# Four small edits to a one-core hybrid mixer block: where the last weights are loaded, a root, a store's queue, and the spacing of side steps

## The chip, the cores and the metric

The program runs on one core of one Trainium2 chip. The metric is the time of one execution on the device in microseconds; of several runs the median counts. The engines have their usual names: PE (TensorE, matmuls), DVE (VectorE), ACT (ScalarE), POOL (GpSimd) and SP, which here only issues DMAs. Each engine works through its own instructions in the order in which they stand in the program, and waits where an operand or a buffer is not ready.

## The reference, cut to what matters

One layer of a hybrid block over 512 latent tokens and 256 context tokens, width 2048, float32:

```
u  = (rms_norm(x)  * (1 + sc)   + sh)   @ w_in      # three head groups read one projection
uc = (rms_norm(ctx) * (1 + sc_c) + sh_c) @ w_in
y_gdn = gated DeltaNet, 6 heads, both directions    # chunked, a triangular solve in each chunk
y_hy  = order-2 Hyena, 512 channels, by FFT
y_ml  = mLSTM, 6 heads, both directions             # matrix memory with exponential gates
x = x + gt * (concat(y_gdn, y_hy, y_ml) @ w_out)    # gt: the gate, a third part of silu(c) @ mod_w
out = x * rsqrt(mean(x * x, -1) + 1e-6) * final_norm
```

## The kernel before

The big products are done at float32 accuracy from halves: a weight tile `raw` (128 x 512) is split into `whi` (a rounded copy by ACT, L275) and `wlo` (the rest, by DVE, L276), and each product is three matmuls of 128 x 512: `xh*whi`, `xl*whi` and `xh*wlo` (L418 to L420; with 256 context columns L427 to L429; in the output projection L1769 to L1771). `raw` has three buffers (RB = 3), `whi` and `wlo` three each (WB = 3). SP issues the load of a piece (L362) when a `raw` buffer is free, that is when the `wlo` of three pieces before is done.

**The middle.** The input projection is a stream of such products, the fill. `weave` (L843) puts the small steps of four chains between them: `gdn` (the DeltaNet heads), `ml_scans` (the mLSTM heads), `gates_row` (the gate) and `convs` (Hyena). A chain yields a pair: the clock units that its step is worth, and the units to wait until its next step. The units are the planner's own clock; a K tile of fill, three matmuls of 512 columns, is worth 0.65. So a pause of LX = 0.5 puts one K tile of fill between two steps, and a pause of 2.0 some four. The planner fixes an order of instructions; it does not see the chip. In `ml_scan` a head of the mLSTM begins with transposes of `kT` and `vT` into PSUM banks of the tag `s` (two buffers), which ACT copies to SBUF (L1486, to `kt` and `v1`, shown as `v`). Then come four scores (L1497, again in `s` banks; ACT takes the exponential, L1500, and DVE the product PT, L1501), then twelve scan steps (L1515 to L1519, in banks of the tag `st`, of which there are three). The solve of the DeltaNet's head runs at the same time; its small DMAs (`mblk`, `ublk`) are issued by ACT, between ACT's activations. It also takes `s` banks: for the transposes of its `vT` (L1364, copied out by ACT as `vr`, L1366), for the 32 x 32 and 64 x 64 products of the inverse. Its scan (L1386, L1393, L1402, L1415) takes two `st` banks at a time. `residual_gate` sums sixteen tiles into `gacc` on DVE (L1571), four times over, and closes each sum with a matmul by a column of ones (L1574).

**The end.** The output projection goes by four blocks of 512 columns, cb = 0 to 3; block 0 is the last of the weave. In blocks 1 and 2 the loop runs over the sixteen K tiles and inside it over four token tiles, so that a piece of weights serves four products. In block 3 the loop runs over the token tiles outside and the K tiles inside, so its sixteen pieces must all be there: thirteen lie in a pool of their own (`wq`), three in the usual buffers. They are drawn from the generator `last_cols`, and before they were drawn in block 2, one behind each K tile 1 to 12, the last four behind the block. `residual` adds the residual, squares it on ACT with a sum over the row into `ss`, and multiplies by the final norm's weights. In block 3 each token tile is closed at once: the sum of squares, its root by `rsqrt1` on DVE (a shift and a subtraction of the bits, then three Newton steps on a tile of 128 x 1), four scalings by ACT and DVE, and four stores of 256 KB by SP (L1855).

Of the kernel before, what the change touches and what calls it, by code (L numbers as in the profile page):

```python
# [10 lines left out]
F32 = mybir.dt.float32  # L11
# [28 lines left out]
LD = 3.5  # L40
LM = 0.5
LX = 0.5
LC = 6.0
LM0 = 1.0
LK = 8.0
# [179 lines left out]
def block_kernel(ctx: ExitStack, tc: tile.TileContext, io, out, dbg=None):  # L225
# [29 lines left out]
    def p_s():  # L255
        return bank("s", 2)
# [83 lines left out]

    def rsqrt1(pool, y, v, tag, bufs):

        i = pool.tile([128, 1], I32, tag=tag, bufs=bufs, name="rs_i")
        DVE.tensor_single_scalar(out=i, in_=v.bitcast(I32), scalar=1, op=ALU.arith_shift_right)
        DVE.tensor_scalar(out=i, in0=i, scalar1=-1, scalar2=0x5F3759DF, op0=ALU.mult, op1=ALU.add)
        w = i.bitcast(F32)
        t = pool.tile([128, 1], F32, tag=tag, bufs=bufs, name="rs_t")
        for c in (3.0, 12.0, 768.0):
            DVE.scalar_tensor_tensor(out=t, in0=w, scalar=v, in1=w, op0=ALU.mult, op1=ALU.mult)
            DVE.scalar_tensor_tensor(out=y, in0=t, scalar=-c, in1=w, op0=ALU.add, op1=ALU.mult)  # L350
            w = y
        DVE.tensor_single_scalar(out=y, in_=y, scalar=-1.0 / 8192, op=ALU.mult)


    wcount = [0]
# [1115 lines left out]
    def ml_scan(h, kT, vT, qT, oT):  # L1471
# [9 lines left out]
        for src, dst in ((kT, kt), (vT, v1)):  # L1481
            for t0, n in ((0, 4), (4, 2)):
                pt = p_s()
                for t in range(n):
                    PE.transpose(pt[:, 128 * t:128 * t + 128], src[:, 128 * (t0 + t):128 * (t0 + t) + 128], ident)
                ACT.activation(out=dst[:, t0:t0 + n, 0:128], in_=pt[:, :128 * n].rearrange("p (t c) -> p t c", c=128),  # L1486
                               func=AF.Copy)
                yield 0.15 * n, LX
        for d in range(2):
            s_ = 1 if d == 0 else -1  # L1490
            paced(POOL.affine_select(out=rows[d], in_=rows[d], pattern=[[0, NL], [s_, 128]], base=0,
# [2 lines left out]
        for j in range(NL):  # L1494
            t = j + NC_
            pk = p_s()
            PE.matmul(pk[:, 0:128], kT[:, 128 * t:128 * t + 128], qT[:, 128 * j:128 * j + 128], start=True, stop=True)  # L1497
            for d in range(2):
                ex = s1.tile([128, 128], F32, tag="ex", bufs=2, name="ex")
                ACT.activation(out=ex, in_=rows[d][:, j], func=AF.Exp, bias=am[:, t, 6 * d + h:6 * d + h + 1])  # L1500
                DVE.tensor_tensor(out=PT[:, d, j], in0=pk[:, 0:128], in1=ex, op=ALU.mult)  # L1501
            yield 0.22, LX
        o_sb = s1.tile([128, NL, 128], F32, tag="mosb", bufs=1, name="osb")
        Cn = [None, None]
        for n in range(NT):
# [53 lines left out]
    def residual_gate():  # L1559

        for b in range(4):
            acc = se.tile([128, 512], F32, tag="gacc", name="gacc")
            for j in range(KT):
                m = wp.tile([128, 512], F32, tag="raw", bufs=RB, name="mg")
                SP.dma_start(out=m, in_=io["mg"][b, j // 2, :, 512 * (j % 2):512 * (j % 2) + 512])
                yield 0, LD
                sk = scol[:, j:j + 1]
                if j == 0:
                    paced(DVE.tensor_single_scalar(out=acc, in_=m, scalar=sk, op=ALU.mult))
                else:  # L1570
                    paced(DVE.scalar_tensor_tensor(out=acc, in0=m, scalar=sk, in1=acc, op0=ALU.mult, op1=ALU.add))  # L1571
                yield 0, LG - LD
            pg = p_s()
            PE.matmul(pg[0:1], ones[:, 0:1], acc, start=True, stop=True)  # L1574
            m = wp.tile([128, 512], F32, tag="raw", bufs=RB, name="mbt")
            SP.dma_start(out=m[0:1], in_=io["mbg"][:, 512 * b:512 * b + 512])
            DVE.tensor_tensor(out=m[0:1], in0=pg[0:1], in1=m[0:1], op=ALU.add)
            SP.dma_start(out=gt_d[:, 512 * b:512 * b + 512], in_=m[0:1])
            yield 0.9, LG
# [227 lines left out]
    fnb = s3.tile([128, D], F32, name="fnb")  # L1807
    POOL.dma_start(out=fnb, in_=io["fnw"].to_broadcast([128, D]))
    ss = s3.tile([128, NL, 4], F32, name="ss3")

    def residual(o, t, cb):
        cs = slice(512 * cb, 512 * cb + 512)
# [5 lines left out]
        ACT.activation(out=xt, in_=rs, func=AF.Square, accum_out=ss[:, t, cb:cb + 1])  # L1818
        if cb < 3:
            DVE.tensor_tensor(out=rs, in0=rs, in1=fnb[:, cs], op=ALU.mult)  # L1820

    wq = outs.enter_context(tc.tile_pool(name="wq", bufs=KT - WB, side="right", reuse_waits="tile"))
    last_cols, ws = w_cols(3, wq), []
    for cb in range(3):
        pt = pt0 if cb == 0 else po_tiles(cb)
        if cb:
            for i, (k, w) in enumerate(zip(ks, w_cols(cb))):
                for t in range(NL):
                    y_product(pt[t], k, t, w)
                if cb == 2 and 0 < i < KT - WB:  # L1830
                    ws.append(next(last_cols))
        for t in range(NL):
            residual(pt[t], t, cb)
# [3 lines left out]
    for t in range(NL):  # L1837
# [2 lines left out]
            y_product(o, k, t, w)  # L1840
        residual(o, t, 3)
        v = s3.tile([128, 1], F32, tag="fv", bufs=2, name="fv")
        DVE.tensor_reduce(out=v, in_=ss[:, t], op=ALU.add, axis=AX.X)
        DVE.tensor_scalar(out=v, in0=v, scalar1=1.0 / D, scalar2=EPS, op0=ALU.mult, op1=ALU.add)
        r = s3.tile([128, 1], F32, tag="fr", bufs=2, name="fr")
        rsqrt1(s3, r, v, "fq", 4)
        for q in (0, 1, 3, 2):
# [4 lines left out]
                ACT.activation(out=rs, in_=rs, func=AF.Copy, scale=r)  # L1852
            else:
                DVE.tensor_single_scalar(out=rs, in_=rs, scalar=r, op=ALU.mult)
            SP.dma_start(out=out[128 * t:128 * t + 128, 512 * q:512 * q + 512], in_=rs)  # L1855
    outs.close()
    cxs.close()
    pss.close()
# [20 lines left out]
```

## Time and profile before

| | |
|---|---|
| median of three runs | 1495.4 us (1494.79 to 1498.05) |
| the profiled execution's own time | 1492.42 us |
| its span, first to last instruction | 1490.6 us |
| PE busy | 1445.4 us (97%) |
| DVE, ACT, POOL busy | 1031.0, 575.1, 215.0 us |
| granted clock of PE | 0.998 of full speed |

The profile is of one execution. Its own time is 1.8 us more than its span, which lies around the first and the last instruction, and 3.0 us less than the median of the runs. A row of PE gives the modelled time of a matmul from its first column in to its last result out, so rows of a stream overlap: the next one starts before the last has ended.

### The profile page before, as it was taken

Reading aid. Unit: us, or ns where it says so; the run is one execution under the profiler, and the core shown is the slowest. Engines: PE = TensorE matmul, PEld = TensorE weight load, DVE = VectorE, ACT = ScalarE, POOL = GpSimd, SP = SyncE. Lnnn points to the kernel's source line nnn. Section 1 sums busy time; section 2 is a strip of 40 time slices with the busy share of each in tenths; the row PEclk is TensorE's granted clock in tenths of the full one; section 3 lists DMA queues with packets and bytes.
Section 4 is the critical chain, followed back from the end, with each engine's and each line's share of the span. In section 5 each row is a group of like instructions: output and inputs, shape, how many; then the busy total and the mean of one; then the engine's idle time right before and its main releaser. Section 6 shows DMA issues by size and latency. Waiting matters only on the chain.

```text
span 1490.6 us, 25062 instructions
## 1 busy us (share of the span) xinstructions
PE 1445.4 (97%) x8822; PEld 1185.2 (80%) x8822; DVE 1031.0 (69%) x2685; ACT 575.1 (39%) x1367; POOL 215.0 (14%) x412
## 2 busy tenths in 40 slices
PE   5999999999999999999999999999999999999997
PEld 1565687888888888888888888888878888888775
DVE  4666776677778787878787767676776677774553
ACT  5433344425242624262335243533353333332431
POOL 2224002112010211020103001200011112210000
PEclk9999999999999999999999999999999999999999
DMA  9999623333344423442344123311322442474542
GB/s 320 318 315 298 218 81 100 102 104 100 100 140 113 123 95 120 125 127 92 124 129 133 65 83 94 110 55 60 86 79 88 163 167 95 149 240 142 169 125 101
DMA packets 145237, 202.82 MB, mean 136 GB/s; under 512 B 57222, under 2 KB 57703, under 8 KB 144856
## 3 DMA queue, kind: packets, MB, share of 16 engines
q1 hardware_dynamic: 89752, 159.50, 32.8%
q0 software_dynamic: 10048, 32.52, 6.9%
q10 hardware_dynamic: 45312, 9.21, 3.2%
q8 instruction: 69, 1.13, 0.3%
q14 instruction: 56, 0.46, 0.1%
HBM read 182.92 MB, written 18.26 MB: 135 GB/s over the span
## 4 chain that ended last, share of the span: by engine, by line
PE 77%; DVE 8%; issue 5%; DMA 5%; ACT 3%; POOL 1%; ACTq 0%; SPq 0%; DVEq 0%; POOLq 0%
PE ml L418 12%; PE ml L420 12%; PE ml L419 12%; PE mc L427 3%; PE mc L428 2%; PE mc L429 2%; PE st L317 2%; DVE wlo L276 2%; PE st L1771 1%; PE st L1770 1%; PE st L1769 1%; DMA raw<-in_wo_dram 1%; PE st L1393 1%; PE st L1402 1%; PE st L323 1%
## 5 line engine op out<-in xcount | busy, mean ns | idle before, releaser
L418 PE MATMUL ml<-xh,whi 128*128 128x512 f32 x1024 | 419.5, 410 | 0.0
L420 PE MATMUL ml<-xh,wlo 128*128 128x512 f32 x1024 | 404.7, 395 | 0.0
L419 PE MATMUL ml<-xs,whi 128*128 128x512 f32 x1024 | 404.5, 395 | 0.0
L275 ACT ACTIVATE whi<-raw 128x512 fp32r<-128x512 f32 x320 | 201.0, 629 | 427.5 <-PE mc L428 150.6
L276 DVE TENSOR_TENSOR wlo<-raw,whi 128x512 fp32r<-128x512 f32 x320 | 221.5, 694 | 177.8 <-ACT whi L275 165.6
L420 PEld LDWEIGHTS ml<-xh,wlo 128*128 128x128 f32 x1024 | 192.5, 188 | 38.9
L418 PEld LDWEIGHTS ml<-xh,whi 128*128 128x128 f32 x1024 | 193.4, 189 | 29.3 <-issue 0.9
L419 PEld LDWEIGHTS ml<-xs,whi 128*128 128x128 f32 x1024 | 193.3, 189 | 27.7
L427 PE MATMUL mc<-cs,whi 128*128 128x256 f32 x384 | 110.7, 288 | 0.0
L428 PE MATMUL mc<-cs,whi 128*128 128x256 f32 x384 | 108.6, 283 | 0.0
L429 PE MATMUL mc<-cs,wlo 128*128 128x256 f32 x384 | 108.3, 282 | 0.0
L427 PEld LDWEIGHTS mc<-cs,whi 128*128 128x128 f32 x384 | 72.6, 189 | 4.1 <-issue 0.9
L428 PEld LDWEIGHTS mc<-cs,whi 128*128 128x128 f32 x384 | 72.3, 188 | 3.1
L429 PEld LDWEIGHTS mc<-cs,wlo 128*128 128x128 f32 x384 | 72.8, 190 | 0.0
L1571 DVE SCALAR_TENSOR_TENSOR gacc<-mg,scol,gacc 128x512 f32<-128x512 f32 x60 | 45.5, 759 | 17.3 <-DMA mg<-in_mg_dram 9.0
L1288 POOL DMA_DIRECT2D G<-rows_d x36 | 19.8, 553 | 217.6 <-DVE T L1154 77.5
L1400 POOL TENSOR_SCALAR ke<-kt,kend 128x128 f32<-128x128 f32 x60 | 24.2, 408 | 150.4 <-PE st L1402 143.6
L1513 POOL TENSOR_SCALAR ke<-kt,wend 128x128 f32<-128x128 f32 x60 | 27.4, 459 | 94.5 <-ACT kt L1486 47.5
L1340 ACT ACTIVATE ex<-G,ngc 128x128 f32<-128x128 f32 x72 | 27.0, 398 | 33.5 <-POOL G L1295 14.3
L1770 PE MATMUL st<-wlo,yh 128*128 128x512 f32 x96 | 37.7, 392 | 0.0
L1771 PE MATMUL st<-whi,yl 128*128 128x512 f32 x96 | 37.7, 392 | 0.0
L1769 PE MATMUL st<-whi,yh 128*128 128x512 f32 x96 | 37.6, 391 | 0.0
(501 smaller groups left out, 2857.4 us busy)
## 6 DMA issues: line engine op xcount, KB each, us to landing
raw<-in_wt_dram SPq DMA_DIRECT2D x256, 256.0 KB, 2.8
mw<-in_mw_dram SPq DMA_DIRECT2D x128, 256.0 KB, 5.8
mg<-in_mg_dram SPq DMA_DIRECT2D x64, 256.0 KB, 2.8
raw<-in_wo_dram SPq DMA_DIRECT2D x64, 256.0 KB, 3.0
fraw<-in_wf_dram SPq DMA_DIRECT2D x16, 320.0 KB, 6.4
G<-rows_d POOLq DMA_DIRECT2D x36, 128.0 KB, 3.3
xs<-in_xT_dram SPq DMA_DIRECT2D x16, 256.0 KB, 5.4
hspec<-hv POOLq DMA_DIRECT2D x16, 256.0 KB, 5.4
```

The lines of the kernel that those rows point to most:

```text
L275: ACT.activation(out=hi, in_=src, func=AF.Copy)
L276: DVE.tensor_tensor(out=lo, in0=src, in1=hi.bitcast(F32), op=ALU.subtract)
L418: PE.matmul(pl[:m], wh, xh[:, kk], start=f, stop=False)
L419: PE.matmul(pl[:m], wh, xl[kk], start=False, stop=False)
L420: stream[0] = PE.matmul(pl[:m], wl, xh[:, kk], start=False, stop=l)
L427: PE.matmul(pc[:m, :CTX], wh, ch[kk], start=f, stop=False)
L428: PE.matmul(pc[:m, :CTX], wh, cl[kk], start=False, stop=False)
L429: stream[0] = PE.matmul(pc[:m, :CTX], wl, ch[kk], start=False, stop=l)
L1571: paced(DVE.scalar_tensor_tensor(out=acc, in0=m, scalar=sk, in1=acc, op0=ALU.mult, op1=ALU.add))
L1769: PE.matmul(o, yh[k][:, ts_], wh, start=f, stop=False)
L1770: PE.matmul(o, yh[k][:, ts_], wl, start=False, stop=False)
L1771: PE.matmul(o, yl[k][:, ts_], wh, start=False, stop=l)
```

## The change

- `last_cols`, the pieces of block 3, are drawn in blocks 1 and 2, behind every second K tile from the sixth on (i = 5, 7, ... 15), six in each block, twelve in all; four are left for the end of block 2, as before.
- `rsqrt1` scales its Newton steps so that the closing multiplication by -1/8192 falls away; the sum of squares of the first three blocks, its division and the epsilon are done when block 2 is closed (`part`), and one instruction joins the fourth block's.
- The store that comes last in each token tile (q = 2, scaled by ACT) is issued by ACT in place of SP.
- The pause behind each step of transposes and of scores in `ml_scan` is LT = 2.0 in place of LX = 0.5 (eight steps in a head), and `residual_gate` pauses LD = 3.5 more before its closing matmul.

```
+LT = 2.0
 def rsqrt1(pool, y, v, tag, bufs):
+    cs = [1.0]
+    for _ in range(3):
+        cs.insert(0, math.copysign((abs(cs[0]) / 2) ** (1.0 / 3), -cs[0]))
...
-    for c in (3.0, 12.0, 768.0):
+    for c in cs[:3]:
         DVE.scalar_tensor_tensor(out=t, in0=w, scalar=v, in1=w, op0=ALU.mult, op1=ALU.mult)
-        DVE.scalar_tensor_tensor(out=y, in0=t, scalar=-c, in1=w, op0=ALU.add, op1=ALU.mult)
+        DVE.scalar_tensor_tensor(out=y, in0=t, scalar=float(np.float32(-3.0 * c * c)), in1=w, op0=ALU.add,
+                                 op1=ALU.mult)
         w = y
-    DVE.tensor_single_scalar(out=y, in_=y, scalar=-1.0 / 8192, op=ALU.mult)
...
 # ml_scan: behind each step of transposes, and behind each score
-                yield 0.15 * n, LX
+                yield 0.15 * n, LT
...
-            yield 0.22, LX
+            yield 0.22, LT
...
 # residual_gate: ahead of the closing matmul
+            yield 0, LD
             pg = p_s()
             PE.matmul(pg[0:1], ones[:, 0:1], acc, start=True, stop=True)
...
 # residual
+        if cb == 2:
+            v = s3.tile([128, 1], F32, tag="fs", bufs=NL, name="fs")
+            DVE.tensor_reduce(out=v, in_=ss[:, t, 0:3], op=ALU.add, axis=AX.X)
+            DVE.tensor_scalar(out=v, in0=v, scalar1=1.0 / D, scalar2=EPS, op0=ALU.mult, op1=ALU.add)
+            part.append(v)
...
 # blocks 1 and 2, behind the products of K tile i
-                if cb == 2 and 0 < i < KT - WB:
+                if i > 3 and i % 2 and len(ws) < KT - WB - 1:
                     ws.append(next(last_cols))
...
 # block 3, the close of a token tile
-        DVE.tensor_reduce(out=v, in_=ss[:, t], op=ALU.add, axis=AX.X)
-        DVE.tensor_scalar(out=v, in0=v, scalar1=1.0 / D, scalar2=EPS, op0=ALU.mult, op1=ALU.add)
+        DVE.scalar_tensor_tensor(out=v, in0=ss[:, t, 3:4], scalar=1.0 / D, in1=part[t], op0=ALU.mult, op1=ALU.add)
...
-            SP.dma_start(out=out[128 * t:128 * t + 128, 512 * q:512 * q + 512], in_=rs)
+            (ACT if q == 2 else SP).dma_start(out=out[128 * t:128 * t + 128, 512 * q:512 * q + 512], in_=rs)
```

The change moves instructions. Lines behind the edits have other numbers after it (L418 to L420 become L425 to L427, L1485 becomes L1492, L1364 becomes L1371, L1393 becomes L1400). PE's order is the same up to the first head's mLSTM. Three places follow.

PE at the start of the fourth head's mLSTM, where `kT` and `vT` are transposed into the two `s` banks; rows of the form `ml<-` are K tiles of fill. Before:

```order
L1485 MATMUL s<-ident,kT 128x128 x4
L418 MATMUL ml<-xh,whi 128x512
L419 MATMUL ml<-xs,whi 128x512
L420 MATMUL ml<-xh,wlo 128x512
L1485 MATMUL s<-ident,kT 128x128 x2
L418 MATMUL ml<-xh,whi 128x512
L419 MATMUL ml<-xs,whi 128x512
L420 MATMUL ml<-xh,wlo 128x512
L1485 MATMUL s<-ident,vT 128x128 x4
```

After, from the second transposes of `kT` on (four K tiles stand ahead of them):

```order
L1492 MATMUL s<-ident,kT 128x128 x2
L425 MATMUL ml<-xh,whi 128x512
L426 MATMUL ml<-xs,whi 128x512
L427 MATMUL ml<-xh,wlo 128x512
L425 MATMUL ml<-xh,whi 128x512
L426 MATMUL ml<-xs,whi 128x512
L427 MATMUL ml<-xh,wlo 128x512
L1371 MATMUL s<-ident,vT 128x128 x6
L425 MATMUL ml<-xh,whi 128x512
L426 MATMUL ml<-xs,whi 128x512
L427 MATMUL ml<-xh,wlo 128x512
L425 MATMUL ml<-xh,whi 128x512
```

The steps of the mLSTM stand further apart, and the DeltaNet's six transposes of its own `vT`, one planner step of four and one of two, come between them with no fill between the two.

PE at the end of the first head's mLSTM scan (L1518 and L1519 before, L1525 and L1526 after: one scan step; `s<-ident,oT` closes the scan). Before, the scan ends ahead of the 64 x 64 products and of the DeltaNet's scan:

```order
L1518 MATMUL st<-v_3599,PT 128x129
L1519 MATMUL st<-Cn,qT 128x129
L418 MATMUL ml<-xh,whi 128x512
L419 MATMUL ml<-xs,whi 128x512
L420 MATMUL ml<-xh,wlo 128x512
L1518 MATMUL st<-v_3599,PT 128x129
L1519 MATMUL st<-Cn,qT 128x129
L418 MATMUL ml<-xh,whi 128x512
L419 MATMUL ml<-xs,whi 128x512
L420 MATMUL ml<-xh,wlo 128x512
L1548 MATMUL s<-ident,oT 128x128 x4
```

After, the DeltaNet's scan (L1400, L1409) has begun:

```order
L1525 MATMUL st<-v_3599,PT 128x129
L1526 MATMUL st<-Cn,qT 128x129
L1400 MATMUL st<-vr,M 128x128 x2
L434 MATMUL mc<-cs,whi 128x256
L435 MATMUL mc<-cs,whi 128x256
L436 MATMUL mc<-cs,wlo 128x256
L434 MATMUL mc<-cs,whi 128x256
L435 MATMUL mc<-cs,whi 128x256
L436 MATMUL mc<-cs,wlo 128x256
L1409 MATMUL st<-u,ke 128x128
L1525 MATMUL st<-v_3599,PT 128x129
L1409 MATMUL st<-u,ke 128x128
```

Over all heads, twelve mLSTM scan steps stand behind the first product of the DeltaNet's scan after the change (2, 3, 3, 2, 2 and 0 in heads 0 to 5), and none before.

SP in blocks 1 to 3 of the output projection; `raw` is a piece of weights, `xt` a tile of the residual. Before:

```order
L1814 DMA xt<-in_xtok_dram 128x512
L362 DMA raw<-in_wo_dram 128x512 x14
L1814 DMA xt<-in_xtok_dram 128x512 x3
L362 DMA raw<-in_wo_dram 128x512 x3
L1814 DMA xt<-in_xtok_dram 128x512
L362 DMA raw<-in_wo_dram 128x512 x23
L1814 DMA xt<-in_xtok_dram 128x512 x5
L1855 DMA out_dram<-res 128x512 x16
```

After:

```order
L1823 DMA xt<-in_xtok_dram 128x512
L369 DMA raw<-in_wo_dram 128x512 x19
L1823 DMA xt<-in_xtok_dram 128x512 x3
L369 DMA raw<-in_wo_dram 128x512 x3
L1823 DMA xt<-in_xtok_dram 128x512
L369 DMA raw<-in_wo_dram 128x512 x18
L1823 DMA xt<-in_xtok_dram 128x512 x5
L1869 DMA out_dram<-res 128x512 x12
```

Five loads have moved ahead of the `xt` tiles of block 1's close, and four stores have left SP.

## Rows read from the trace of the kernel before

**Rows 1.** The page's first part: busy time and share of PE.

```profile
PE 1445.4 (97%) x8822; PEld 1185.2 (80%) x8822; DVE 1031.0 (69%) x2685; ACT 575.1 (39%) x1367; POOL 215.0 (14%) x412
```

**Rows 2.** Windows by stage: length, then busy time of PE, PEld, DVE, ACT, POOL.

```profile
230.00:1342.00 1112.00, 1102.55 (x7073) 941.67 (x7072) 808.97 (x2177) 427.85 (x1076) 164.93 (x331) 1.00 0.37 113
1342.00:1390.00 48.00, 48.00 (x213) 39.77 (x212) 23.32 (x38) 16.07 (x32) 0.00 (x0) 1.00 0.41 134
1390.00:1436.00 46.00, 43.95 (x184) 33.90 (x184) 23.93 (x38) 18.20 (x31) 0.00 (x0) 1.00 0.54 171
1480.00:1490.64 10.64, 0.00 (x0) 0.00 (x0) 4.28 (x15) 2.06 (x4) 0.00 (x0) 0.65 0.29 99
```

**Rows 3.** PE's waits, 200 to 1340 us: total, times, longest.

```profile
PE s L1485 <- ACT kt L1486: 3.2, 3, 1.8
PE s L1574 <- DVE gacc L1571: 1.4, 2, 0.8
PE s L1364 <- DVE PT L1501: 0.7, 2, 0.6
...
PE s L1497 <- DVE PT L1501: 0.6, 2, 0.5
...
PE s L1497 <- ACT vr L1366: 0.3, 2, 0.2
```

**Rows 4.** Timeline of PE, fourth head's mLSTM: start, length, idle before.

```profile
793.03 0.40 PE L420 MATMUL ml<-xh,wlo 128*128 128x512 f32 x1
794.66 0.66 PE L1485 MATMUL s<-ident,vT 128*128 128x128 f32 x4 [1.24 <-ACT kt L1486]
```

**Rows 5.** Timeline of ACT beside it.

```profile
792.50 0.38 ACTq L1188 DMA_DIRECT2D U<-ublk  x1
793.00 0.63 ACT L275 ACTIVATE whi<-raw 128x512 fp32r<-128x512 f32 x1 [3.65 <-PE s L1485]
...
794.02 0.86 ACT L1486 ACTIVATE kt<-s 128x512 f32<-128x512 f32 x2
```

**Rows 6.** Groups by line, whole span: busy, mean ns; then idle before.

```profile
L1532 DVE SCALAR_TENSOR_TENSOR nm<-st,wint,nm 128x129 f32<-128x129 f32 x48 | 16.7, 349 | 5.5 <-ACT nm L1531 4.7
L1527 DVE SCALAR_TENSOR_TENSOR Cn<-Cn,mdec,st 128x129 f32<-128x129 f32 x48 | 16.4, 344 | 3.8 <-PE st L1519 3.0 <-PE st L1515 0.5
```

**Rows 7.** Waits of PE, then of SP's queue, 1385 to 1436 us.

```profile
PE ml L1769 <- ACT whi L275: 1.2, 2, 0.9
PE ml L1770 <- DVE wlo L276: 0.7, 3, 0.2
...
SPq L362 <- DVE wlo L276: 24.2, 26, 1.4
```

**Rows 8.** Groups by line in the same stretch.

```profile
L276 DVE TENSOR_TENSOR wlo<-raw,whi 128x512 fp32r<-128x512 f32 x29 | 19.9, 692 | 22.5 <-ACT whi L275 22.5
L275 ACT ACTIVATE whi<-raw 128x512 fp32r<-128x512 f32 x29 | 18.3, 632 | 28.2 <-DMA raw<-in_wo_dram 22.1 <-PE s L1771 3.9 <-DVE wlo L276 1.5
```

**Rows 9.** DMA issues of the whole span: KB each, median us to landing.

```profile
raw<-in_wo_dram SPq DMA_DIRECT2D x64, 256.0 KB, 3.0
```

**Rows 10.** Timeline of DVE, the last token tile's root.

```profile
1482.09 0.16 DVE L1843 TENSOR_REDUCE fv<-ss 128x1 f32<-128x4 f32 x1 [0.84 <-ACT xt L1818]
1482.28 0.15 DVE L1844 TENSOR_SCALAR fv<-fv 128x1 f32<-128x1 f32 x1
...
1484.00 0.16 DVE L350 SCALAR_TENSOR_TENSOR fr<-rs_t,fr 128x1 f32<-128x1 f32 x1
1484.19 0.15 DVE L352 TENSOR_SCALAR fr<-fr 128x1 f32<-128x1 f32 x1
```

**Rows 11.** Windows of the last stores; the last two columns are DMA share and GB/s.

```profile
1486.50:1487.50 1.00, 0.00 (x0) 0.00 (x0) 0.00 (x0) 0.00 (x0) 0.00 (x0) 0.50 1.10 356
1487.50:1488.50 1.00, 0.00 (x0) 0.00 (x0) 0.00 (x0) 0.00 (x0) 0.00 (x0) 0.50 1.04 348
```

**Rows 12.** The store's line: shortest, median and longest time of one issue, in ns.

```profile
L1855 SPq DMA_DIRECT2D out_dram<-res x16: 332/388/407, 1451.3 to 1486.3; - x16
```

More of the change, by code (lines that the diff above doesn't have):

```diff
@@ L341, in rsqrt1 @@
     def rsqrt1(pool, y, v, tag, bufs):
+        cs = [1.0]
+        for _ in range(3):
+            cs.insert(0, math.copysign((abs(cs[0]) / 2) ** (1.0 / 3), -cs[0]))
         i = pool.tile([128, 1], I32, tag=tag, bufs=bufs, name="rs_i")
         DVE.tensor_single_scalar(out=i, in_=v.bitcast(I32), scalar=1, op=ALU.arith_shift_right)
-        DVE.tensor_scalar(out=i, in0=i, scalar1=-1, scalar2=0x5F3759DF, op0=ALU.mult, op1=ALU.add)
+        DVE.tensor_scalar(out=i, in0=i, scalar1=-1, op0=ALU.mult, op1=ALU.add,
+                          scalar2=0x5F3759DF + int(2 ** 23 * math.log2(-cs[0])) - 2 ** 31)
         w = i.bitcast(F32)
         t = pool.tile([128, 1], F32, tag=tag, bufs=bufs, name="rs_t")
-        for c in (3.0, 12.0, 768.0):
+        for c in cs[:3]:
             DVE.scalar_tensor_tensor(out=t, in0=w, scalar=v, in1=w, op0=ALU.mult, op1=ALU.mult)
-            DVE.scalar_tensor_tensor(out=y, in0=t, scalar=-c, in1=w, op0=ALU.add, op1=ALU.mult)
+            DVE.scalar_tensor_tensor(out=y, in0=t, scalar=float(np.float32(-3.0 * c * c)), in1=w, op0=ALU.add,
+                                     op1=ALU.mult)
             w = y
-        DVE.tensor_single_scalar(out=y, in_=y, scalar=-1.0 / 8192, op=ALU.mult)
     wcount = [0]
@@ L1809, in block_kernel @@
     ss = s3.tile([128, NL, 4], F32, name="ss3")
+    part = []
     def residual(o, t, cb):
```

## The prediction

> **What bounds the kernel now.** I read the busy times first. PE is busy 1445.4 us [rows 1] of a span of 1490.6, so 45.2 us are all that any edit here can win, unless it takes PE's own work away, and none does: the number of matmuls stays. So the next view is the one by stage, for where PE is idle [rows 2]. From 230 to 1342 us, the weave, it is idle for 1112.00 - 1102.55 = 9.45 us. From 1342 to 1390, block 1 of the output projection, it is never idle. From 1390 to 1436, block 2, it is idle for 46.00 - 43.95 = 2.05 us, and behind its last matmul there is a tail of 10.64 us without PE. That makes 22.1 us; the rest lies in the two stretches not shown, block 3 and above all the first 230 us, in which PE's order is not changed.
>
> Who ended PE's idle time in the weave is told by its waits [rows 3]: the mLSTM's transposes 3.2 us in 3 waits, its scores 0.6 + 0.3 us in 4, the DeltaNet's transposes waiting for the mLSTM's PT 0.7 us in 2, the gate's closing matmul 1.4 us in 2. That is 6.2 of the 9.45 us, and all of it stands at steps that the change spaces out. In block 2 the waits are for `whi` and `wlo` [rows 7].
>
> A wait costs more than it shows. In the timeline [rows 4] the matmul at 793.03 lasts 0.40 us, and the next in a stream starts about 0.23 us behind it (block 1: 213 recorded matmuls in 48.00 us make 0.225 [rows 2]). The next one started at 794.66, so 1.63 - 0.23 = 1.40 us were lost, where 1.24 is shown. I add 0.16 us for each wait.
>
> **The mLSTM's spacing.** The `s` banks are two, and the transposes of `vT` need the bank that ACT empties by copying `kt`. At 794 us ACT was idle for 3.65 us until just behind the issue of the DMA `U<-ublk` at 792.50, and the copies came only at 794.02 [rows 5]: ACT works in order, and it was held at a small DMA of the DeltaNet's solve. Before, two K tiles of fill stand between the filling of the first bank and its next use, which was due at 793.03 + 0.23 = 793.3 and came 1.4 us late. After, the next use of that bank is L1371, with six K tiles ahead of it: four more of 3 x 0.225 = 0.68 us, so it is due at 793.3 + 2.7 = 796.0. That outlasts the hold, since the copies end at 794.02 + 0.86 = 794.9. The scores need ACT twice and DVE twice before a bank is free again, and get 2.7 us in place of 0.7. Gain: 3.2 + 0.6 + 0.3 + 0.7 = 4.8 us shown, in 9 waits, so 4.8 + 9 x 0.16 = **6.2 us**. The fill is only moved from elsewhere in the stream and costs nothing of itself.
>
> **The gate's pause.** Its closing matmul comes 3.5 units later, some five K tiles or 3.7 us, where the longest wait was 0.8 us. Gain 1.4 + 2 x 0.16 = **1.7 us**. The four pauses make the gate end some 15 us later in all. Its result is read first by the `residual` of block 0, behind the whole weave; that is the cover, and PE would pay the 15 us only if the gate were the last chain to end, which `convs` is.
>
> **The weights of block 3.** A K tile in blocks 1 and 2 is 12 matmuls, 12 x 0.225 = 2.7 us. In block 2 two pieces are asked for in that time, one each 1.35 us. A piece holds its `raw` buffer for the load, 3.0 us [rows 9], the split by ACT, 0.63, and by DVE, 0.69 [rows 8]. With three buffers that is one each 4.32 / 3 = 1.44 us, longer than 1.35; and SP waited for `wlo` 26 times, 24.2 us in all [rows 7]. So the weights fall behind, and PE waits 5 times. After the change both blocks ask for three pieces in two K tiles at most, one each 1.8 us, which is over 1.44, and the first five K tiles of a block, in which `residual` fills DVE, ask for one alone. So block 2's loss goes: 2.05 + 5 x 0.16 = **2.9 us**. What block 1 takes on is hidden by its slack: it ran one piece in 2.7 us without an idle PE.
>
> **The root.** In the tail each small DVE instruction starts 0.19 us behind the one before: the reduction at 1482.09 and its scaling at 1482.28, the last Newton step at 1484.00 and the closing multiplication at 1484.19 [rows 10]. Two become one and one falls away: 2 x 0.19 = **0.4 us**, on the path that ends the program. The three other tiles' roots lie beside PE's stream. The new sums in block 2's close are 8 instructions, 8 x 0.19 = 1.5 us of DVE, ahead of the last piece's `wlo`. That piece is wanted by the sixteenth K tile of the first token tile, 15 x 3 x 0.225 = 10 us into block 3. I cost it at nothing; without that cover it is 1.5 us.
>
> **The store by ACT.** The fourth store no longer waits for SP's third issue, 0.39 us [rows 12]. But in the two windows in which the last stores are written the DMA engines are busy 1.10 and 1.04 of their time, at 356 and 348 GB/s [rows 11]. They are full, and one that starts earlier only queues there. So 0, with 0 and 0.4 as bounds. The Trainium skill's page DMA: Bandwidth & Descriptors, section "Issuing engines are not separate DMA queues", says that DMAs of all issuing engines run on the same sixteen engines and interleave, so that a second issuer saves its issue time alone; the full engines of those windows agree. By the page the store could give the one issue time at the most.
>
> Together 6.2 + 1.7 + 2.9 + 0.4 = 11.2 us.
>
> **What comes in its place.** Two things, which the trace of before doesn't show. First, twelve mLSTM scan steps now stand inside the DeltaNet's scan, none before. Each puts two instructions of 0.35 us on DVE [rows 6] between those that PE waits for in the other scan, so 0 to 12 x 0.69 = 8.3 us. DVE is busy 809 of 1112 us in the weave [rows 2], so most of it finds a hole; the nearest rows, scores that wait behind the other chain's `vr` on ACT, cost 0.3 us in 2 waits [rows 3], 0.15 each. I take 2.0 us. Second, the DeltaNet's six transposes now stand between the mLSTM's in five heads, and need both `s` banks at once: 0 to 0.6 us each, the longest such wait of L1364 or L1497 being 0.6 [rows 3], so 0 to 3.0. I take 0.2 each, 1.0 us. Net gain 11.2 - 3.0 = 8.2 us: 1492.4 becomes 1484.2. The median of the runs lay 3.0 us above the profiled execution, so I predict **1487 us**.
>
> **Rivals.**
>
> *The waits only move.* The hold of ACT is made by a DMA that lands when it lands, and the change takes nothing from it. Another user of an `s` bank could stand there now, and the L1371 row of six transposes is such a user. Then the 6.2 us are not won: 1.7 + 2.9 + 0.4 - 3.0 = 2.0, so 1493.4 us, which is no change. For it: the hold lasts 3.65 us, and one bank pair serves all. Against it: each use of a bank now has more fill ahead of it in every head. Chance 0.17.
>
> *All is won and nothing new waits.* 11.2 us and up to 0.4 by the store: 1484 us. For it: the scan steps of both chains show no waits of note before. Chance 0.20.
>
> *The weights don't catch up.* If the load takes 3.0 us alone but over 4.1 with the residual's tiles beside it, three buffers give one piece in 1.8 us and block 2 stays as it is, with block 1 joining it: 2.9 us less, 1490 us. Against it: block 1 ran with DMA at 134 GB/s, block 2 at 171 [rows 2], and the last stores at 356. Chance 0.07.
>
> *Slower: the two scans hold each other up.* The DeltaNet's scan takes two of the three `st` banks and the mLSTM's steps the third, so each step's matmuls wait until DVE has read the step before, and the DeltaNet's next matmul stands behind them on PE. If each of the twelve steps costs more than (11.2 - 1.0) / 12 = 0.85 us, more than its 0.69 us of DVE, the gain is gone; at 1.2 us it is 12 x 1.2 + 1.0 - 11.2 = 4.2 us slower, 1499.6 us. Chance 0.08.
>
> **How the numbers follow.** My forecast has 0.48, and the four rivals 0.52. A measurement of this kernel can tell about 0.2%, 3 us, from no change, so faster means under 1492.4. Of the forecast 0.46 lies there; with 0.20, 0.07 and 0.04 of the first rival faster has 0.77. Slower has 0.08 and 0.01 of the first rival, no change the other 0.14. The range goes from all won, 1484, less 2 us for waits too short to show, to both unknown costs at their upper ends, 8.3 + 3.0 = 11.3 against 11.2, which is 1495: **1482 to 1495**. It leaves out the slower rival and the ends.
>
> **What would show it.** PE's waits should have no row of L1492 or L1582 with more than a few tenths, and L1504 under 0.5 us; block 2's window should have no idle PE; the last root should take 9 instructions of DVE; the last stores' windows should again be full. New rows for L1371, L1393, L1400, L1409 or L1525 are the price of the spacing. I am wrong if PE's idle time from 230 to 1342 us stays at 9 us, or if block 2 still waits for `whi`.

## The result, and the profile after

The changed kernel takes 1488.07 us (median of 6, 1485.43 to 1491.43) beside 1495.1 for the kernel before (median of 6, 1493.38 to 1498.05): a ratio of 0.995, 95% interval 0.9933 to 0.9966, so 7.0 us faster. The forecast was 1487. Its profiled execution took 1485.43 us, with a span of 1483.5 in place of 1490.6.

The starts of the first products of each stage, read in PE's timeline of both profiles, say where the 7.15 us of span went (us):

| stretch | before | after | difference |
|---|---|---|---|
| start to the first DeltaNet products (`s<-kT`) | 275.9 | 276.7 | +0.8 |
| weave, from there to block 0 | 1011.3 | 1007.1 | -4.2 |
| block 0 of the output projection | 56.1 | 57.7 | +1.5 |
| block 1 | 43.52 | 43.52 | 0 |
| block 2 | 48.45 | 43.52 | -4.9 |
| block 3, to the start of its last matmul | 44.08 | 44.36 | +0.3 |
| from there to the end | 11.23 | 10.63 | -0.6 |

The 48.45 us of block 2 hold two matmuls that are not its own. In the kernel before they are block 3's first two, and they stand early in PE's order, where block 3's first weights are drawn:

```profile
1393.22 0.40 PE L1769 MATMUL st<-whi,yh 128*128 128x512 f32 x1
1393.46 0.40 PE L1770 MATMUL st<-wlo,yh 128*128 128x512 f32 x1
```

Block 3 is shorter by the same two. At 0.23 us each that leaves 4.5 us that block 2 lost of itself, and the two blocks together won 4.65 us.

PE has the same 8822 instructions as in [rows 1], and of the span 1483.5 - 1441.0 = 42.5 us are left without it, 45.2 before:

```profile
PE 1441.0 (97%) x8822; PEld 1188.8 (80%) x8822; DVE 1017.1 (69%) x2685; ACT 576.6 (39%) x1367; POOL 213.2 (14%) x412
```

The windows by stage, which answer to [rows 2] (length, busy time of PE, PEld, DVE, ACT, POOL, granted clock, DMA share, GB/s); blocks 1 and 2 begin some 2 us earlier, and their two windows lie 7 us earlier:

```profile
230.00:1335.00 1105.00, 1096.55 (x7053) 940.96 (x7053) 795.17 (x2178) 429.42 (x1075) 162.72 (x331) 1.00 0.37 112
1335.00:1383.00 48.00, 48.00 (x214) 39.75 (x213) 23.18 (x36) 17.71 (x32) 0.00 (x0) 1.00 0.59 188
1383.00:1429.00 46.00, 46.00 (x205) 38.09 (x204) 24.88 (x39) 17.17 (x33) 0.00 (x0) 1.00 0.48 150
```

Block 2 has no idle PE any more and passes 205 matmuls in the 46.00 us in which it passed 184. The weave is the surprise: PE is still idle for 1105.00 - 1096.55 = 8.45 us, against 9.45. These two windows take in different shares of block 0; in the weave alone, from the first DeltaNet products to block 0, the idle time went from 9.24 to 7.60 us, and in block 0 from 0.05 to 0.69. PE's waits, 200 us to the end, tell why (total, times, longest), beside [rows 3]:

```profile
PE s L1492 <- ACT vr L1373: 1.8, 4, 1.1
PE s L1582 <- DVE M L1349: 1.5, 1, 1.5
PE s L1342 <- DVE M L1349: 1.5, 2, 0.9
...
PE ml L427 <- DVE wlo L277: 0.7, 1, 0.7
PE ml L1778 <- DVE wlo L277: 0.5, 1, 0.5
```

The four kinds of wait that the forecast meant to remove (`kt` 3.2 us, the scores 0.9, PT 0.7, the gate's `gacc` 1.4) are gone but for 0.2 us of the scores. In their place the mLSTM's transposes wait for the DeltaNet's `vr`, the gate's closing matmul for an `s` bank, and the next head's `kT` products for a bank too: 4.8 us in three rows, of which the last had 0.6 before (there L1335). No row of the scans (L1393, L1400, L1409, L1522, L1525) is among them.

The tail, in a timeline of DVE, ACT and the two issuing queues, beside [rows 10, 12]:

```profile
1475.49 0.16 DVE L1858 SCALAR_TENSOR_TENSOR fv<-ss,fs 128x1 f32<-128x1 f32 x1 [0.79 <-ACT xt L1827]
...
1477.21 0.16 DVE L357 SCALAR_TENSOR_TENSOR fr<-rs_t,fr 128x1 f32<-128x1 f32 x1
1477.40 1.34 ACT L1866 ACTIVATE res<-res,fr 128x512 f32<-128x512 f32 x2 [1.95 <-DVE fr L357]
...
1477.91 1.30 SPq L1869 DMA_DIRECT2D out_dram<-res  x3
1478.77 0.36 ACTq L1869 DMA_DIRECT2D out_dram<-res  x1
```

The root takes 1477.40 - 1475.49 = 1.91 us; before, it took 1484.38 - 1482.09 = 2.29 (its last row of [rows 10] starts 0.19 us ahead of 1484.38). From the first scaling to the end it is 1483.49 - 1477.40 = 6.09 us, and 1490.64 - 1484.38 = 6.26 before. While the last stores are written the DMA engines are as full as in [rows 11] (the last two columns are DMA share and GB/s):

```profile
1479.00:1480.00 1.00, 0.00 (x0) 0.00 (x0) 0.00 (x0) 0.00 (x0) 0.00 (x0) 0.50 1.05 379
1480.00:1481.00 1.00, 0.00 (x0) 0.00 (x0) 0.00 (x0) 0.00 (x0) 0.00 (x0) 0.50 1.07 352
```

### The profile page after: what moved, and what is told of

It is laid out like the page before. It is cut to its first block, busy times and chain, and to the rows that moved or that the text cites. A ratio compares the mean times of both kernels' runs of the same rounds, so it can differ in the third digit from the quotient of the medians.

```text
span 1483.5 us, 25078 instructions
## 1 busy us (share of the span) xinstructions
PE 1441.0 (97%) x8822; PEld 1188.8 (80%) x8822; DVE 1017.1 (69%) x2685; ACT 576.6 (39%) x1367; POOL 213.2 (14%) x412
## 4 chain that ended last, share of the span: by engine, by line
PE 67%; issue 3%; DVE 3%; DMA 2%; ACT 2%; POOL 1%; SPq 0%; DVEq 0%; POOLq 0%; ACTq 0%
PE ml L425 12%; PE ml L427 12%; PE ml L426 12%; PE mc L434 2%; PE mc L435 2%; PE mc L436 2%; PE st L1778 1%; PE st L1779 1%; PE st L1777 1%; PE st L1522 1%; PE st L1400 1%; PE st L1409 1%; PE st L1393 1%; PE st L1525 1%; PE st L324 1%
## 5 line engine op out<-in xcount | busy, mean ns | idle before, releaser
L425 PE MATMUL ml<-xh,whi 128*128 128x512 f32 x1024 | 416.3, 407 | 0.0
L427 PE MATMUL ml<-xh,wlo 128*128 128x512 f32 x1024 | 404.7, 395 | 0.7 <-DVE wlo L277 0.7
L427 PEld LDWEIGHTS ml<-xh,wlo 128*128 128x128 f32 x1024 | 192.5, 188 | 40.6 <-DVE wlo L277 1.6
L425 PEld LDWEIGHTS ml<-xh,whi 128*128 128x128 f32 x1024 | 193.3, 189 | 31.3 <-issue 1.7
L434 PE MATMUL mc<-cs,whi 128*128 128x256 f32 x384 | 112.9, 294 | 0.0
L435 PE MATMUL mc<-cs,whi 128*128 128x256 f32 x384 | 109.8, 286 | 0.0
L1578 DVE SCALAR_TENSOR_TENSOR gacc<-mg,scol,gacc 128x512 f32<-128x512 f32 x60 | 45.2, 753 | 35.8 <-DMA mg<-in_mg_dram 32.1
L1520 POOL TENSOR_SCALAR ke<-kt,wend 128x128 f32<-128x128 f32 x60 | 23.9, 400 | 119.8 <-PE st L1522 67.6
L1349 DVE SCALAR_TENSOR_TENSOR M<-s,nd,ex 128x128 f32<-128x128 f32 x72 | 24.0, 346 | 20.1 <-PE s L1344 11.4
```

What stands on the lines that cost most here:

```text
L425: PE.matmul(pl[:m], wh, xh[:, kk], start=f, stop=False)
L427: stream[0] = PE.matmul(pl[:m], wl, xh[:, kk], start=False, stop=l)
L434: PE.matmul(pc[:m, :CTX], wh, ch[kk], start=f, stop=False)
L435: PE.matmul(pc[:m, :CTX], wh, cl[kk], start=False, stop=False)
```

## The experiments

Three questions: whether block 2's loss came from the fetch of block 3's weights and why it was larger than forecast; what the two kinds of spacing are worth, each and together, and what the new waits are made of; and why block 0 gave 1.5 us back. A theory is that of its expectation; single executions stand beside one execution of the kernel before on the same chip. All kernels computed the whole result.

### The weights of block 3

`old_fetch`: the changed kernel with the former condition.

```
-                if i > 3 and i % 2 and len(ws) < KT - WB - 1:
+                if cb == 2 and 0 < i < KT - WB:
```

> The changed kernel with block 3's weights drawn in block 2 again, one behind each of K tiles 1 to 12. Theory (three raw buffers cannot pass two pieces in 2.7 us): block 2 takes 48.0 to 48.6 us again instead of 43.5, PE waits there for whi or wlo about 5 times, and the span is 4.5 to 5 us longer than with the change, about 1488. Rival (block 2 lost its time to something that the other edits removed too, such as where the weave ends): block 2 stays under 45 us.

It took 1493.0 us (the kernel before 1495.86), with a span of 1491.1 where 1488 was expected. Block 2 went from 43.52 to 48.97 us, and its PE waits are those of [rows 7] again:

```profile
PE ml L1777 <- ACT whi L276: 2.0, 2, 1.0
PE ml L1778 <- DVE wlo L277: 0.7, 3, 0.2
```

They show 2.7 us; 5.45 are gone, of which 0.46 are the two early matmuls of block 3, so 5.0 are lost. PE's timeline at one of the waits (start, length, idle before) shows a part of the rest:

```profile
1398.85 0.39 PE L1779 MATMUL s<-whi,yl 128*128 128x512 f32 x1
1400.25 0.49 PE L1777 MATMUL ml<-whi,yh 128*128 128x512 f32 x1 [1.02 <-ACT whi L276]
1400.98 0.50 PE L1778 MATMUL ml<-wlo,yh 128*128 128x512 f32 x1 [0.23 <-DVE wlo L277]
1401.32 0.40 PE L1779 MATMUL ml<-whi,yl 128*128 128x512 f32 x1
```

In a stream a matmul starts 0.23 us behind the last. Here the steps are 1.40, 0.73 and 0.34, so 2.47 - 3 x 0.23 = 1.78 us are lost where 1.02 + 0.23 = 1.25 are shown: 0.27 hidden for each of these two waits. Some of what is lost shows as no wait at all: in the kernel before, block 2 has 14 steps of 0.33 us or more, which together are 4.3 us longer than 0.23 each, and the waits' list has five of them.

`own_raw`: `old_fetch`, with three `raw` buffers of its own for block 3's pieces.

```
+            raw = (wp if pool is None else rq[0]).tile([128, 512], F32, tag="raw", bufs=RB, name="raw")
...
+    rq.append(outs.enter_context(tc.tile_pool(name="rq", bufs=RB, side="right", reuse_waits="tile")))
```

> As the run before, the old fetch in block 2, but block 3's pieces are loaded into three raw buffers of their own. Theory (the three buffers set the pace, 4.3 us for three): with six buffers for two streams the pace is 0.72 us for a piece, so PE doesn't wait in block 2, which takes 43.5 to 44.0 us although the loads stand where they stood. Rival (the DMA engines, or ACT and DVE with two splits for each K tile, are too slow): block 2 stays at 47 to 48.5 us, with waits for whi and wlo as before.

A miss as a kernel: 1499.67 us (before 1495.86). Block 2 ran without a wait, 43.52 us, but block 0 took 63.5 and block 1 46.5, with PE's longest waits now there (1288 to 1442 us):

```profile
PE ml L1779 <- DVE wlo L277: 2.7, 2, 2.4
PE st L1779 <- DVE wlo L277: 2.6, 1, 2.6
```

With buffers free from the start, the loads of block 3 were no longer paced by block 2's products and came among those of blocks 0 and 1; in block 2 itself 16 pieces were split where `old_fetch` split 28. So it doesn't prove that the buffers were block 2's limit. It shows that the loss follows the place where the twelve extra pieces are loaded and split. Block 0's time is not all theirs: behind its wait of 2.4 us the clock was granted at half for 3.4 us (the last section has a like case). For the buffers speaks the pace that the traces show: 10 to 40 us into block 2 SP issued a load each 1.48 us in the kernel before, and each 1.42 to 1.51 in the other four profiles with the old fetch there. The forecast had 1.44 for three buffers. That is an argument, not an experiment.

### The spacing

`spacing_alone`: the kernel before with LT in the two places of `ml_scan` (the first fence) and nothing else. `gate_alone`: the kernel before with the gate's pause (the second) and nothing else. `no_gate`: the changed kernel without that line.

```
-                yield 0.15 * n, LX
+                yield 0.15 * n, LT
...
-            yield 0.22, LX
+            yield 0.22, LT
```

```
                 yield 0, LG - LD
+            yield 0, LD
```

> The kernel before with the mLSTM's wider spacing alone. Theory (the spacing takes away about 6 us of waits at transposes and scores and brings 3 us back at the banks that DeltaNet's transposes and products share): the weave, from the first DeltaNet products at 276 us to block 1, takes 2.5 to 4.5 us less than before (1067.4), the gate's two waits stay. Rival (the weave's gain of 2.7 us came from the gate's pause or from chance in the order): within 1 us of before.

1491.35 us (before 1495.86). The weave to block 0 took 1006.8 us, 4.5 less than in the kernel before. But the expectation spoke of the stretch to block 1, and there it is 1065.8 against 1067.4, 1.7 less, which neither the theory nor the rival has: block 0 took 59.0 us in place of 56.1. Nor did the gate's two waits stay; both were gone without the pause, and what stood in place of `gacc` was one wait of 0.5 us.

> The changed kernel without the gate's longer pause. Theory (the pause took away 1.4 us of waits and put one of 1.5 us at another gate matmul, which now stands between the DeltaNet's first products and waits for their bank): the weave is within 1 us of the changed kernel's, the 1.5 us wait is gone and waits for gacc of 1 to 2 us are back. Rival (the pause wins its 1.7 us and the other wait is of the spacing): the weave is 1.5 to 2 us longer than with the change.

1488.51 us (before 1495.86). The weave took 1007.2 us, no more than with the pause, though the waits changed their names. The wait of 1.5 us went, but `gacc` did not come back, as the theory had it; the gate's closing matmul (here L1581) waits 0.9 us for a bank. PE's waits there:

```profile
PE s L1371 <- ACT kt L1493: 1.9, 2, 1.5
PE s L1492 <- ACT vr L1373: 1.8, 3, 1.4
...
PE s L1581 <- DVE kt L1315: 0.9, 1, 0.9
```

> The kernel before with the gate's pause alone. First theory (the forecast's term): the 1.7 us that TensorE waited in 4 for the gate's gacc rows are gone and nothing comes for them, so the stretch from the first DeltaNet products to block 0 is 1011.3 - 1.7 = 1009.6 us and the time about 1493.8. Rival: what the gate's row product waited for was shifted by the later start of everything around it, and the pause only moves the product to another wait; then the stretch stays at 1011 +/- 0.5 and the time within 1 us of the kernel before, as leaving the pause out of the changed kernel (stretch 1007.2 against 1007.1) suggests.

1494.48 us (before 1499.81 on that chip). The weave took 1010.4 us, between the theory and its rival: 0.9 less than before. The gate waited for nothing, and the mLSTM's transposes waited more, where [rows 3] have 3.2:

```profile
PE s L1485 <- ACT kt L1486: 4.5, 3, 1.8
```

So in these two orders the pause is worth 0 to 0.9 us in the weave, not 1.7. One execution each does not part that from the scatter told below: with the spacing, the weave takes 1006.8 and 1007.2 us in the two profiles without the pause, and 1007.1 or more in the seven with it.

### What the new wait is made of

In the changed kernel the DeltaNet's six transposes L1371 follow one another without fill and take both `s` banks; the mLSTM's next transposes, L1492, wait until ACT has copied them (`vr`). `sp_store`, whose purpose was another (below), shows it at its worst. ACT's timeline (start, length, idle before), then PE's:

```profile
799.44 0.37 ACT L1493 ACTIVATE kt<-s 128x256 f32<-128x256 f32 x1
803.15 0.63 ACT L276 ACTIVATE whi<-raw 128x512 fp32r<-128x512 f32 x1 [3.35 <-DMA raw<-in_wt_dram]
...
803.94 1.59 ACT L1373 ACTIVATE vr<-s,nk 128x128 f32<-128x128 f32 x6
```

```profile
805.09 0.66 PE L1492 MATMUL s<-ident,vT 128*128 128x128 f32 x4 [2.58 <-ACT vr L1373]
```

The transposes L1371 were done by 801.4; but in ACT's order a copy `whi` stands ahead of `vr`, its weight tile had not landed, and ACT stood for 3.35 us. The row of PE names `vr`; what was late is a load that neither step reads. In the changed kernel's own profile the same copy waited 1.15 us and PE 0.29. The landing time of the weights' loads around it is 3.5 us there (median of 7, 788 to 803 us) and 5.2 in `sp_store` (median of 6, 790 to 806).

Over seven profiles with this order of the weave, PE waited at this one place 0.3, 0.7, 1.6, 1.6, 1.7, 1.7 and 2.6 us, and the weave took 1007.1 to 1009.7 us in six of them and 1012.2 in `sp_store`.

`vt_apart`: the changed kernel, with DeltaNet's steps L1371 paced too.

```
             for t in range(n):
                 ACT.activation(out=vr[:, t0 + t], in_=pt[:, 128 * t:128 * t + 128], func=AF.Copy,
                                scale=nk[:, t0 + t:t0 + t + 1])
-            yield 0.15 * n, 0.0
+            yield 0.15 * n, LT
```

> The changed kernel with the two DeltaNet transposes of a step (L1371) paced by LT as well, so that they do not stand behind one another between the mLSTM's. Theory: the wait of L1492 for vr, 1.8 us in 4, comes from these transposes standing together with the mLSTM's; it goes to under 0.5 us and the stretch to block 0 becomes about 1005.5 us. Rival: PE has no other step ready at these places, so as much is waited for at another line (kt, PT or a bank) and the stretch stays at 1007 +/- 0.5 us or grows.

1481.6 us (before 1499.81): the weave took 1002.2 us, 4.9 less than in the changed kernel. The 1499.81 us beside it lie above the kernel before's other times (1493.38 to 1498.05), so it was then timed again, beside the changed kernel, `old_fetch` and a version without the gate's pause, all on one chip, where the kernel before took 1495.64 us (15 executions).

> The changed kernel as it is, timed on the same chip as the three kernels beside it, so that they can be set against it. Theory: 0.995 of the kernel before, as measured (0.9933 to 0.9966). Part of the scatter between executions is the clock: where TensorE stood 2.58 us for vr in one kernel, it was granted 1.2 GHz for the 3.3 us from 806.5 us on; so slower executions should show a lower mean granted clock than the fastest (0.998).

> The changed kernel with block 3's weights drawn in block 2 again, now timed. Theory (block 2 lost 4.7 to 5 us to the late wlo, not the 2.9 us of the forecast): 4.5 to 5.5 us slower than the changed kernel on the same chip. Rival (the forecast's price of 0.16 us hidden for each wait): 2.9 us.

> The changed kernel with DeltaNet's transposes L1371 paced by LT as well, timed. Theory: what the trace of one execution showed (1002.2 us to block 0 in place of 1007.1, L1492 without a wait) holds in the time: 4 to 6 us faster than the changed kernel on the same chip, 0.991 to 0.992 of the kernel before. Rival: the one execution was a lucky one and the times agree within 2 us.

> The same without the gate's pause. Theory: the pause is worth nothing of its own; where the rest of the weave is spread wider, the gate's rows are ready in any case, and the two kernels agree within 1.5 us. Rival: the forecast's term, 1.7 us slower without the pause.

| kernel | median, us (n) | to the kernel before, 95% interval | weave in its profile | block 2 |
|---|---|---|---|---|
| changed kernel again | 1487.77 (5) | 0.9941, 0.9927 to 0.9955 | 1009.6 | 43.52 |
| `old_fetch_timed` | 1494.03 (11) | 0.9986, 0.9976 to 0.9996 | 1009.7 | 47.77 |
| `vt_apart_timed` | 1480.85 (4) | 0.9898, 0.9884 to 0.9911 | 1001.5 | 43.52 |
| `vt_apart_no_gate` | 1485.43 (5) | 0.9928, 0.9915 to 0.994 | 1006.3 | 43.52 |

The version with the DeltaNet's transposes apart is faster than both kernels: 1487.77 - 1480.85 = 6.9 us under the changed one, somewhat more than expected. PE is idle for 3.06 us in its weave, 9.21 in the profile of the changed kernel beside it. No wait of L1492 is left, which had 3.1 us there, and none of L1582, which had 1.5; what the edit did to the second was not parted from the first. PE's waits (270 to 1283 us):

```profile
PE s L1342 <- DVE M L1349: 0.7, 2, 0.4
PE st L324 <- ACT O L276: 0.7, 1, 0.7
PE st L1522 <- DVE Cn L1531: 0.6, 1, 0.6
```

The place again, ACT and then PE: the six transposes are now four and two. Three K tiles of fill stand behind the first four, then come the mLSTM's four with the other two right behind them. Each copy by ACT comes in time, though it still stands behind a `whi` that waits for its load.

```profile
794.22 1.14 ACT L1373 ACTIVATE vr<-s,nk 128x128 f32<-128x128 f32 x4
796.12 0.63 ACT L276 ACTIVATE whi<-raw 128x512 fp32r<-128x512 f32 x1 [0.75 <-DMA raw<-in_wt_dram]
...
797.23 0.62 ACT L1373 ACTIVATE vr<-s,nk 128x128 f32<-128x128 f32 x2
```

```profile
793.59 0.60 PE L1371 MATMUL s<-ident,vT 128*128 128x128 f32 x4
796.10 0.60 PE L1492 MATMUL s<-ident,vT 128*128 128x128 f32 x4
796.54 0.38 PE L1371 MATMUL s<-ident,vT 128*128 128x128 f32 x2
```

`old_fetch_timed` is 1494.03 - 1487.77 = 6.3 us behind the changed kernel, more than the theory's 4.5 to 5.5 and far from the rival's 2.9.

With the gate's pause taken out of it, `vt_apart_timed` loses 1485.43 - 1480.85 = 4.6 us. That is against my theory that the pause is worth nothing, and more than the rival's 1.7. Its waits (same stretch) have the gate's back:

```profile
PE s L1342 <- DVE M L1349: 1.4, 2, 1.0
PE s L1581 <- DVE rs_t L337: 1.4, 1, 1.4
PE st L324 <- ACT O L276: 1.3, 1, 1.3
```

1.4 us of it is the gate's; 0.7 more for `kT` and 0.6 more for `O` are of other steps, whose place in the order moved with it, and behind the 1.3 us for `O` (PE's row at 1209.29) the clock was granted at half for 3.4 us, as told in the last section, some 1.6 us of the 4.6 if the other executions have it too, which no profile shows. What an edit of the order is worth thus depends on the other edits: the same pause gave 0 to 0.9 us in two orders and 4.6 in the third.

### Block 0, and the store

`gt_pieces`: the changed kernel, with the load of `gtb` in four pieces on SP's queue.

```
-    gtb = s3.tile([128, D], F32, name="gtb")
-    POOL.dma_start(out=gtb, in_=gt_d.to_broadcast([128, D]))
+    gtb = [s3.tile([128, 512], F32, name=f"gtb{b}") for b in range(4)]
...
+        if t == 0:
+            SP.dma_start(out=gtb[cb], in_=gt_d[:, cs].to_broadcast([128, 512]))
```

> The changed kernel with the 1 MB load of gtb on POOL's queue in the middle of block 0 (issued 1319.4 us, landing 6.8 us later) taken apart into four 256 KB pieces on SP's queue, issued behind block 0's weights. Theory: block 0 lost its time because zt, 256 KB on ACT's queue, shares the DMA engines with gtb; DVE stood 2.3 us for zt and the wlo behind it came late. Without it zt lands in time, PE has no wait for wlo at 43 us into the block, and block 0 takes 55.7 to 56.2 us in place of 57.7. Rival: zt is late by the weights' own loads or its issue, which stay; then block 0 takes 57 to 59 us as in the other kernels with the spacing. The pieces that now stand before block 1's weights may cost block 1 up to 2 us.

The theory fell. 1486.1 us (before 1499.81), block 0 58.1 us, and DVE waited for `zt` 2.15 us beside 2.25 in the changed kernel, with no `gtb` on the way. Block 1 took 44.0 us, 0.45 more, with the pieces ahead of its weights. The issue of that `zt` by ACT, and the row of DVE that read it (idle before):

```profile
1324.79 0.33 ACTq L1751 DMA_DIRECT2D zt<-zd  x1
```

```profile
1329.37 0.75 DVE L1756 SCALAR_TENSOR_TENSOR yr<-hy,hnw,zt 128x512 f32<-128x512 f32 x1 [2.15 <-DMA zt<-zd]
```

4.6 us from issue to use, while the weights' loads run beside it. Block 0 took 57.3 to 59.4 us in every profile but `own_raw`'s and the one of the kernel before (56.1); 58.3 in `gate_alone`, which has the gate's pause and none of the other edits. So the 1.5 us that the comparison puts on block 0 may well be that one execution's; this was not tried further.

`sp_store`: the changed kernel with all stores issued by SP.

```
-            (ACT if q == 2 else SP).dma_start(out=out[128 * t:128 * t + 128, 512 * q:512 * q + 512], in_=rs)
+            SP.dma_start(out=out[128 * t:128 * t + 128, 512 * q:512 * q + 512], in_=rs)
```

> The changed kernel with all stores on SP's queue again. Theory: ACT's queue saves only the issue time of one store; from the first scaling to the end 6.26 us as before in place of 6.09, so 0.15 to 0.2 us more behind the last matmul (10.8 in place of 10.63). Rival: the four last stores are bound by the DMA engines and the end stays at 10.63 +/- 0.05. A single time can't show it; the rows behind the last matmul do.

Its time, 1491.12 us (before 1499.81), has the wait shown above in it and says nothing of the store. Behind its last matmul come 10.79 us, counted from the start of that matmul, where nine profiles with ACT's store and `gtb` in one piece lie between 10.62 and 10.67: the store gives 0.12 to 0.17 us, with a single profile on the one side. The Trainium skill's page DMA: Bandwidth & Descriptors, section "Issuing engines are not separate DMA queues", allows a second issuer its issue time at the most, 0.39 us by [rows 12]; these runs agree.

## Why the prediction was right

The time was 1.1 us from the forecast, and the profiled execution 1.2 us from the 1484.2 of the sum. That it came so near is in part luck: the fetch gave 1.8 us more than its term, while the weave gave 0.7 us less than its own, and block 0 and the start took back 1.5 and 0.8 us that no term has.

**What bounds the kernel** held: PE's idle time was what could be won. The reading of its size did not. "I add 0.16 us for each wait" was worked out at one wait and is not a constant: block 2 lost 4.5 us of itself with 2.05 shown in 5 waits, 0.5 for each.

**The weights.** Mechanism right (`old_fetch` brings the waits back, the new fetch makes block 2 43.52 us in eight profiles of eight that have it; that three `raw` buffers are the reason was argued, not isolated), size wrong: forecast 2.9, measured 4.65 over blocks 2 and 3 in the two first profiles. In the five profiles with the old fetch in block 2, `own_raw` aside, it takes 46.47, 47.13, 47.77, 48.45 and 48.97 us; without the two early matmuls that is a loss of 2.5 to 5.0. In medians it was 6.3 us, while the two profiled executions, 1493.95 and 1489.76 us, are 4.2 apart, as their block 2s are: the changed kernel's was the slowest of its five, 2.0 over its median, so the other 2 us is not shown to be the fetch's. The step that failed is the price of a wait: 5 x 0.16 = 0.8 us were forecast as hidden, and 2.4 were. A late matmul is followed by a step of 0.34 us too, and some come late without a listed wait; [rows 2] had the better count: 184 matmuls by 0.225 make 41.4 us, so 4.6 of that window's 46.00 us were lost. Block 1's slack did cover the pieces in the first pair; in one later profile (`after_again`) block 1 took 44.3 us, with a wait of 0.5 us for `wlo`.

**mLSTM's spacing, gate and what comes in their place**: 6.2 + 1.7 - 3.0 = 4.9 was forecast for the weave. Measured 4.2 in the first pair of profiles; the six profiles of this order in which the clock did not fall in the weave lie 1.6 to 4.2 under the one of before. The steps behind the sum are half right. The waits named did go, and as the forecast had it: ACT was still held, idle for 3.58 us up to 794.66 in the changed kernel's timeline (3.65 in [rows 5]), and no transposes waited for `kt`. Of the two things that come in their place, the mLSTM's scan steps inside the DeltaNet's cost nothing that shows (forecast 2.0; none of the scan rows waits). The DeltaNet's six transposes between the mLSTM's cost more than the forecast 1.0: L1492's wait for `vr` is 1.8 to 3.8 us a profile, and the banks for L1582 and L1342 took 2.5 to 3.0 more, 0.6 of it there before. No term of the forecast prices these two rows. The forecast said that L1492 and L1582 would show no more than a few tenths: wrong. It also said that I would be wrong if PE stayed idle for 9 us in the weave: it stayed at 8.45, so the first rival, waits that only move, holds for most of what was shown. Of the weave's 4.2 us, 1.6 are shown idle time (9.24 to 7.60) and the rest is time in which PE counts as busy. I did not find out of what kind that is. That the order around the six transposes is the cause of the new waits was shown by pacing them: 1487.77 to 1480.85 us.

**The gate's pause**, forecast 1.7: 0 to 0.9 in two orders, 4.6 in the third.

**The root**: forecast 0.4, measured 2.29 - 1.91 = 0.38. **The store**: forecast 0 with 0.4 as the bound, measured 0.12 to 0.17, though the engines were as full as before (1.05 and 1.07 of their time in the two windows). Why it gave anything is not shown.

**The rivals.** The two scans did not hold each other up, the weights did catch up, and not all was won, since the three rows of new waits make 4.8 us.

## What to carry to other kernels

Where a stream of equal matmuls is interrupted, count the matmuls in a window and multiply by their pitch; the idle time that waits show was about half of what was lost here (2.05 of 4.5 us). When steps of two chains share two banks and one in-order engine empties them, spread both chains, not one: the wait goes to whichever still stands packed. A wait that names a copy is to be followed to what stands ahead of that copy on its engine, here a load for quite another step.

## What the runs showed of the hardware

A wait can cost twice. Behind the 2.58 us that PE stood in `sp_store` its granted clock fell to half, 1.2 GHz in place of 2.4. Windows of 1 us there (the clock is the third column from the end), and PE's timeline in them:

```profile
806.00:807.00 1.00, 1.00 (x4) 0.75 (x4) 0.13 (x1) 0.99 (x4) 0.00 (x0) 0.51 0.88 299
807.00:808.00 1.00, 1.00 (x4) 0.79 (x3) 0.00 (x0) 0.65 (x3) 0.00 (x0) 0.50 0.33 127
...
809.00:810.00 1.00, 1.00 (x5) 0.77 (x4) 0.41 (x1) 0.44 (x2) 0.00 (x0) 0.78 0.00 0
```

```profile
806.48 0.63 PE L427 MATMUL ml<-xh,wlo 128*128 128x512 f32 x1
806.91 0.63 PE L425 MATMUL ml<-xh,whi 128*128 128x512 f32 x1
```

The matmuls start 0.43 us apart in place of 0.23, for some 3.4 us, so about 1.6 us are lost behind a wait of 2.58. In `vt_apart_no_gate` the same came behind 1.35 us: the windows from 1209 to 1213 us show 0.72, 0.50, 0.50 and 0.58. Not each wait is followed by it. One and the same wait of 1.75 us (`ml<-xh,fhi`) ends between 46.8 and 48.6 us in all fourteen profiles; within 1.5 us behind it the clock fell to half in five of them, for 3.4 us each, and in the other nine it stayed. PE's order up to there is the same in all of them, so neither the wait nor the order alone decides it. In the 15 executions of the kernel before beside the last four kernels, the six with a mean clock of 0.998 took 1495.3 us on average and the three at 0.996 or under 1497.7. It doesn't explain all of the scatter, as I had expected: the slowest of the changed kernel's five, 1489.76, ran at 0.998.

The landing time of the 256 KB loads around 800 us had a median of 3.5 us in the changed kernel's profile and 5.2 in `sp_store`, which has the same order there. ACT, which empties the PSUM bank, stood at such a load for 1.15 and 3.35 us, and PE's waits behind it, 0.29 and 2.58 us, differ by as much.
